# A hybrid encoder layer: one fixed instruction order for the second sweep, its GLA product in three passes, and two-operand work moved from VectorE to GpSimd

## The chip, the cores and the metric

The kernel runs on one core of a Trainium2 chip. A core has a matrix engine (PE, TensorE), a vector engine (DVE, VectorE), an activation engine (ACT, ScalarE), a general engine (POOL, GpSimd), and a queue that issues most DMAs (SP, SyncE). Each works through its own instruction queue in order; semaphores tie them together. The metric is the device time of one execution in microseconds (us).

## The reference, cut to what matters

The layer projects x (2048 x 1024) once and feeds two token mixers: four heads of bidirectional gated linear attention (GLA, decayed scans forward and backward), and four heads of softmax attention with compressed q and kv (MLA). Their gated outputs are joined, projected and normalised.

```python
h = x @ w_in                      # q,k,v,gate,lr_f,lr_b | cq, ckv, kr, gate
# GLA, per chunk and head; b = cumsum(log decay)
o_inter = (q * exp(b)) @ state    # state: decayed sum of k^T v of the chunks before
o = rms_norm(o_fwd + o_bwd, norm_g) * silu(gate)
# MLA
q  = rms_norm(cq) @ w_uq ;  kv = rms_norm(ckv) @ w_ukv   # rope on part of q and on kr
p  = softmax(q_nope k_nope^T + q_rope k_r^T) ;  o = (p @ v) * silu(gate)
x  = layer_norm(alpha * x + concat(o_a, o_b) @ w_out)
```

All is float32. Every large product is computed from splits: a = ah + al, where ah is a rounded copy (`hi`, on ACT) and al the remainder (`lo`, a subtraction of two operands, on DVE or POOL). `mm3` sums ah bh + ah bl + al bh.

## The kernel before, in words

Four stages. **Sweep A** goes over the 16 chunks of 128 tokens from last to first: GLA projections, the part of GLA inside a chunk and the backward state, all stored to HBM (`qd_s`, `oi_s`, `su_s`, and `u_s` for silu of the gate). **Late gates** computes the gates of chunks 15 and 14 and loads the second sweep's weights. **Sweep C**, the second sweep, goes forward, in 8 steps of two chunks; here the change lies. **Attention** then runs 16 blocks of scores, softmax and product, in an order written out by hand (`PLACE`), and ends with the output projection.

In sweep C each chunk c has two halves of work. MLA (`ml_*`, L890 to L950): `ipm` = x times the latent weights (24 matmuls, 448 wide); squares and `rsqrt` (the root comes from Ln and Exp on ACT, then four tiny DVE operations, L160 to L165); normalised `cq`, `ckv`; rope on `kr`; four transposes `tm`, copied to high and low parts; `pqr` and its rope; transposes `tq`. GLA (`gb_*`, L825 to L889): loads `SU`, `qdb`, `oib`, `ub`; the forward state `Sf` times a decay into `Mb` (L846, DVE), `Sf` advanced on POOL (L848, L849); highs and lows of q (`qhb`, `qlb`) and of the joined states (`MMb`, two 64-partition pieces each); the product `Ob` (L865, L866); its norm, the gate (`og`), four transposes `ot` and the store. Per step there are also `pz` (the MLA gate, 96 matmuls, 256 wide) with its silu `gm`, and `pq` (q absorbed into the compressed space, 24 matmuls).

The product reads

```python
mm(Op[:, h], qh[:, h], MM[:, h], start=True, stop=False)        # 256 wide: high and low of MM
mm(Op[:, h, 0], ql[:, h], MM[:, h, 0], start=False, stop=True)  # 128 wide
V.tensor_tensor(oi, Op[:, :, 0], oi, ALU.add)                   # then the second half too
```

so its sum is moved to SBUF (`oib`) by two DVE additions, and the PSUM buffer is free after the second.

Program order is given by hooks between the matmuls (`lat`, `zhooks`); the framework's scheduler then arranges the instructions of each engine by priority and readiness, with a few `after` and `high_priority` hints. PSUM in sweep C is three pools of two buffers: `ip` (ipm), `tr` (transposes, pqr), `gp` (Ob, pz, pq). x of both chunks of a step is held in one pair of tiles (`xch`, `xcl`), so x of the next step can be split only when ipm and pz of this one have read it.

Of the kernel before, what the change touches and what calls it, by code (L numbers as in the profile page):

```python
# [9 lines left out]
F32 = mybir.dt.float32  # L10
# [8 lines left out]
P = 128  # L19
# [81 lines left out]

def _trunc(v, bits):

    m, e = math.frexp(v)
    h = math.ldexp(math.floor(m * 2 ** bits), e - bits)
    return h, v - h


class K:
# [43 lines left out]
    def rsqrt(self, pool, u, n, name):  # L153

        nc = self.nc
        l = pool.tile([P, n], F32, tag=f"rs_l{n}", name=f"{name}_l")
        y = pool.tile([P, n], F32, tag=f"rs_y{n}", name=f"{name}_y")
        t = pool.tile([P, n], F32, tag=f"rs_t{n}", name=f"{name}_t")
        r = pool.tile([P, n], F32, tag=f"rs_r{n}", name=f"{name}_r")
        nc.scalar.activation(l, u, AF.Ln)  # L160
        nc.scalar.activation(y, l, AF.Exp, scale=-0.5)
        nc.vector.tensor_tensor(t, y, y, ALU.mult)
        nc.vector.tensor_tensor(t, t, u, ALU.mult)
        nc.vector.tensor_scalar(t, t, -0.5, 1.5, ALU.mult, ALU.add)
        nc.vector.tensor_tensor(r, y, t, ALU.mult)  # L165
        return r

# [105 lines left out]

    def setup_q(self, w1, ps):

        nc, ins, bc = self.nc, self.ins, self.bc
        for t, n in ((self.gkv_c, "gkv_col"), (self.gn_c, "gn_col")):
            nc.sync.dma_start(t, ins[n])
        gq = bc.tile([P, 2], F32, name="gq")
        nc.sync.dma_start(gq, ins["gq_col"])  # L280
        gkv_b = w1.tile([P, P], F32, tag="ckv", name="gkv_b")
        nc.sync.dma_start(gkv_b, ins["gkv_bc"])
        t1 = w1.tile([P, 2, 512], F32, tag="qa", name="wkr")
        wkT = t1[:, 0].rearrange("p (h l) -> p h l", h=H)
        wqr = t1[:, 1].rearrange("p (c d) -> p c d", c=2)
        nc.sync.dma_start(wqr, ins["wqr"])
        nc.sync.dma_start(wkT, ins["wkT"])
        wqT = w1.tile([P, H, 256], F32, tag="gm", name="wqT")
        nc.sync.dma_start(wqT, ins["wqT"])
        nc.vector.tensor_scalar(gq, gq, QK_SCALE, None, ALU.mult)  # L290
        yield
        for ct in range(2):
            nc.scalar.activation(wqr[:, ct], wqr[:, ct], AF.Copy, scale=gq[:, ct:ct + 1])
        self.hi(self.wqr_h, wqr)
        self.lo(self.wqr_l, wqr, self.wqr_h, "pool")
        for ct in range(2):
            yield
            pa = ps.tile([P, 512], F32, tag="tr", name=f"pabs{ct}")
            for h in range(H):
                nc.tensor.matmul(pa[:, h * P:(h + 1) * P], wqT[:, h, ct * P:(ct + 1) * P], wkT[:, h], start=True,  # L300
                                 stop=True)
            wa = w1.tile([P, H, P], F32, tag="og", name=f"wabs{ct}", bufs=2)
            nc.vector.scalar_tensor_tensor(
                wa, pa.rearrange("p (h l) -> p h l", h=H), gq[:, ct:ct + 1],
                gkv_b[:, None, :].to_broadcast([P, H, P]), ALU.mult, ALU.mult)
            self.hi(self.wabs_h[:, ct], wa)
            self.lo(self.wabs_l[:, ct], wa, self.wabs_h[:, ct], "pool")
        yield
# [195 lines left out]
    def gate(self, c, xh, xl, pool, wide=False):  # L504

        if wide:
            pg = self.gp.tile([P, 2, 512], F32, tag="gp", name=f"ipg{c}")[:, 0]
        else:
            pg = self.ip.tile([P, 512], F32, tag="ip", name=f"ipg{c}")
        for k in range(NK):  # L510
            self.mm3(pg, xh[:, k, 0], xl[:, k, 0], self.wgate[k][0], self.wgate[k][1],
                     start=(k == 0), stop=(k == NK - 1))
        u = self.silu(pool, pg, [P, 512], "gs" if pool is not self.wl else "ub", f"{c}")
        self.store(c).dma_start(self.u_s[c], u)
# [169 lines left out]
    def sweep_c(self):  # L684

        tc, nc, ins = self.tc, self.nc, self.ins
        with ExitStack() as ctx:
            w1 = ctx.enter_context(tc.tile_pool(name="wk2", bufs=1, reuse_waits="tile"))
            sm = ctx.enter_context(tc.tile_pool(name="smc", bufs=2, reuse_waits="tile"))
            ip, tr, gp = self.ip, self.tr, self.gp  # L690
            Wm, Wz = self.Wm, self.Wz
            NST = NCH // 2
            Sf = w1.tile([64, H, P], F32, name="Sf")
            nc.vector.memset(Sf, 0.0)
            xh, xl, split = self.xch, self.xcl, self.split_c
            x2 = lambda t, k: t[:, k].rearrange("p a t -> p (a t)")
            G = [dict(c=c, Sf=Sf, w1=w1, sm=sm, tr=tr, gp=gp) for c in range(NCH)]
            self.gb_load(G[0])
            with tc.high_priority(300):
                self.gb_prep(G[0])  # L700
            setup = self.setup_q(w1, tr)
            next(setup)
            L = None
            for st in range(NST):
                qb, qo = st // 2, (st % 2) * 256
                c0, c1 = 2 * st, 2 * st + 1
                cqT_h = w1.tile([P, 2, 2, P], F32R, tag="cqT_h", name=f"cqT_h{st}")
                cqT_l = w1.tile([P, 2, 2, P], F32R, tag="cqT_l", name=f"cqT_l{st}")
                qrT = []
                cur = [dict(c=c, j=j, st=st, cqT_h=cqT_h, cqT_l=cqT_l, qrT=qrT, w1=w1, sm=sm, tr=tr)  # L710
                       for j, c in enumerate((c0, c1))]
                if st < NST - 1:
                    xs = self.load_x(st + 1, "xc", 2)

                def lat(j, hooks):
                    c = cur[j]["c"]
                    pm = ip.tile([P, 512], F32, tag="ip", name=f"ipm{c}")
                    for k in range(NK):
                        self.mm3(pm[:, :448], xh[:, k, j], xl[:, k, j], Wm[k][0], Wm[k][1],
                                 start=(k == 0), stop=(k == NK - 1))  # L720
# [12 lines left out]
                hooks = {3: [lambda: self.gb_inter(G[c0])]}
                zhooks = {k: [] for k in range(8)}
                if L is not None:
                    P1 = L
                    zhooks[0] += [lambda: self.ml_T(P1)]
                    zhooks[1] += [lambda: self.ml_q(P1)]
                    zhooks[2 if last else 3] += [lambda: self.ml_qT(P1)]
                    zhooks[2 if last else 3] += [lambda: self.absorb(P1), lambda: self.store_qr(P1), lambda: self.gb_out(G[c0 - 1])]  # L740
                else:
                    for k in (1, 3, 5):
                        zhooks[k] += [lambda: next(setup)]
                self.gb_load(G[c1])
                lat(0, hooks)
                self.gb_norm(G[c0])
                if last:
                    self.gb_prep(G[c1])
                    lat(1, {3: [lambda: self.gb_inter(G[c1])]})
                    self.gb_norm(G[c1])  # L750
                    zhooks[2] += [T0]
                    zhooks[3] += [lambda: self.gb_out(G[c0])]
                    zhooks[4] += [q0, T1]
                    zhooks[5] += [qT0, lambda: self.gb_out(G[c1])]
                    zhooks[6] += [q1]
                else:
# [692 lines left out]
```

## Time and profile before

| | |
|---|---|
| median of 3 runs | 1382.49 us (1380.39 to 1384.55) |
| the profiled execution, and its span | 1379.36 us, 1377.5 us |
| mean granted TensorE clock | 0.989 |
| sweep C, first ipm to the first scores | 395.24 to 671.70 us |

The page gives busy time by engine, 40 equal slices of the span, DMA queues, the chain of work that ended last, and the costliest groups of instructions: line, engine, operation, output<-inputs with shapes and count, then busy time and the mean of one in ns, then the idle time of the engine before them with what ended it. A timeline row is start, length, engine, line, operation. Line L123 is the helper `lo`, L117 the helper `hi`, L149 to L151 are `mm3`.

### The profile page before, as it was taken

What the parts mean: (1) busy time and instruction counts of PE and PEld (TensorE: products, weight loads), DVE (VectorE), ACT (ScalarE), POOL (GpSimd) and SP (SyncE); (2) the same over time, 40 slices, a digit from 0 to 9 for tenths busy, and PEclk for the clock granted to TensorE, in tenths of its full rate; (3) what the DMA queues carried; (4) which work ended last, traced back from release to release, by engine and by line L of the source; (5) the groups of instructions that cost most, each with busy time, mean ns of one, the idle gap of its engine ahead of it and who ended that gap; (6) DMA issues with size and microseconds to landing.
All of it is one profiled execution on the core that took longest, in us unless ns stands there. A gap on an engine that the chain in (4) does not pass through costs nothing.

```text
span 1377.5 us, 19847 instructions
## 1 busy us (share of the span) xinstructions
PE 1312.2 (95%) x7056; PEld 1137.9 (83%) x7056; DVE 1013.1 (74%) x1829; ACT 826.2 (60%) x1353; POOL 727.1 (53%) x394
## 2 busy tenths in 40 slices
PE   6899999999998999899999999999999999999997
PEld 6889898989887888888878888888888887787875
DVE  7747755555688777777588888888888888578676
ACT  6555556546575555555577878788888888511110
POOL 3442423232432332232058878889999999745442
PEclk9899999999999999999999999999999999999999
DMA  7222222222384555553711211111112210366973
GB/s 251 81 62 78 62 77 81 81 62 77 107 288 125 183 176 171 165 169 101 238 45 22 57 39 39 39 54 55 54 54 85 65 52 9 87 212 198 182 180 121
DMA packets 108963, 147.38 MB, mean 107 GB/s; under 512 B 17886, under 2 KB 63326, under 8 KB 108864
## 3 DMA queue, kind: packets, MB, share of 16 engines
q1 hardware_dynamic: 99696, 143.98, 35.5%
q0 software_dynamic: 672, 2.10, 0.4%
q10 hardware_dynamic: 8496, 0.03, 0.3%
q8 instruction: 56, 0.92, 0.3%
q14 instruction: 43, 0.35, 0.1%
HBM read 94.93 MB, written 51.15 MB: 106 GB/s over the span
## 4 chain that ended last, share of the span: by engine, by line
PE 50%; DVE 8%; issue 4%; ACT 3%; POOL 2%; DMA 2%; SPq 1%; DVEq 0%; POOLq 0%; ACTq 0%
PE o L149 4%; PE o L151 4%; PE o L150 4%; PE pS L1000 4%; PE pS L1003 4%; PE pS L1002 4%; PE pS L1004 4%; PE pS L1001 4%; PE po L151 1%; PE po L150 1%; PE po L149 1%; DVE MMb L123 1%; PE ipm L149 1%; PE ipm L150 1%; PE ipm L151 1%
## 5 line engine op out<-in xcount | busy, mean ns | idle before, releaser
L123 POOL TENSOR_TENSOR pl<-s,ph 128x1024 fp32r<-128x1024 f32 x128 | 307.1, 2416 | 66.8 <-ACT ph L117 60.4
L1022 DVE TENSOR_TENSOR rm<-pS,rm 128x512 f32<-128x512 f32 x210 | 144.8, 690 | 44.6 <-ACT s L1009 39.5
L1009 ACT ACTIVATE s<-pS 128x1024 f32<-128x1024 f32 x128 | 131.3, 1027 | 67.4 <-PE pS L1004 64.9
L1046 DVE TENSOR_TENSOR s<-s,mb 128x1024 f32<-128x1024 f32 x128 | 151.1, 1212 | 9.2 <-PE mb L1040 9.2
L117 ACT ACTIVATE ph<-s 128x1024 fp32r<-128x1024 f32 x128 | 135.0, 1057 | 16.7 <-PE o L151 16.1
L1050 ACT ACTIVATE s<-s 128x1024 f32<-128x1024 f32 x128 | 131.4, 1050 | 13.5 <-DVE s L1046 13.4
L149 PE MATMUL ipa<-wah,xah 128*128 128x384 f32 (+1 forms) x384 | 131.5, 342 | 6.3 <-ACT wah L117 6.3
L151 PE MATMUL ipa<-wah,xal 128*128 128x384 f32 (+1 forms) x384 | 126.6, 330 | 0.0
L150 PE MATMUL ipa<-wal,xah 128*128 128x384 f32 (+1 forms) x384 | 125.6, 327 | 0.0
L645 POOL TENSOR_TENSOR Us<-Us,cw 128x512 f32<-128x512 f32 x16 | 18.2, 1137 | 202.0 <-DVE Us L642 172.6
L1000 PE MATMUL pS<-qh,ckvT_h 128*128 128x512 f32 x256 | 103.9, 406 | 2.4 <-ACT s L1009 1.7
L149 PE MATMUL o<-ph,vh 128*128 128x512 f32 x256 | 102.6, 401 | 0.0
L151 PE MATMUL o<-ph,vl 128*128 128x512 f32 x256 | 101.3, 396 | 0.0
L1003 PE MATMUL pS<-rh,krs 128*128 128x512 f32 x256 | 101.2, 395 | 0.0
L150 PE MATMUL o<-pl,vh 128*128 128x512 f32 x256 | 101.1, 395 | 0.0
L1002 PE MATMUL pS<-qh,ckvT_l 128*128 128x512 f32 x256 | 100.8, 394 | 0.0
L1004 PE MATMUL pS<-rl,krs 128*128 128x512 f32 x256 | 100.7, 393 | 0.0
L1001 PE MATMUL pS<-ql,ckvT_h 128*128 128x512 f32 x256 | 100.6, 393 | 0.0
L1073 DVE TENSOR_TENSOR ap<-ap,s 128x512 f32<-128x512 f32 x120 | 83.1, 692 | 6.3 <-ACT s L1050 4.4
L149 PEld LDWEIGHTS ipa<-wah,xah 128*128 128x128 f32 x384 | 74.2, 193 | 7.0 <-ACT wah L117 6.3
L123 POOL TENSOR_TENSOR ol<-of,oh 128x512 fp32r<-128x512 f32 x32 | 43.6, 1361 | 68.8 <-ACT oh L117 58.8
L150 PEld LDWEIGHTS ipa<-wal,xah 128*128 128x128 f32 x384 | 74.2, 193 | 1.0 <-DVE wal L123 0.4
(319 smaller groups left out, 3899.1 us busy)
## 6 DMA issues: line engine op xcount, KB each, us to landing
xcf<-xT_dram SPq DMA_DIRECT2D x16, 512.0 KB, 4.1
xr<-x_dram SPq DMA_DIRECT2D x16, 512.0 KB, 6.1
out_dram<-rr SPq DMA_DIRECT2D x32, 256.0 KB, 2.9
xaf<-xT_dram SPq DMA_DIRECT2D x14, 512.0 KB, 4.3
SU<-su_s SPq DMA_DIRECT2D x16, 256.0 KB, 3.5
qdb<-qd_s SPq DMA_DIRECT2D x16, 256.0 KB, 4.1
oib<-oi_s SPq DMA_DIRECT2D x16, 256.0 KB, 2.8
ub<-u_s SPq DMA_DIRECT2D x16, 256.0 KB, 3.0
```

Of the source, the lines that this page charges most:

```text
L117: return nc.scalar.activation(dst, src, AF.Copy).ins
L123: return e.tensor_tensor(dst, src, hi.bitcast(F32), ALU.subtract).ins
L149: mm(out, ah, bh, start=start, stop=False)
L150: mm(out, ah, bl, start=False, stop=False)
L151: mm(out, al, bh, start=False, stop=stop)
L1000: mm(ps[:, e], kh, qh, start=True, stop=False)
L1001: mm(ps[:, e], kh, ql, start=False, stop=False)
L1002: mm(ps[:, e], kl, qh, start=False, stop=False)
L1003: mm(ps[:, e], kr, rh, start=False, stop=False)
L1004: mm(ps[:, e], kr, rl, start=False, stop=True)
L1022: V.tensor_tensor(d["rm"], src[:, e], d["rm"], ALU.max)
L1046: V.tensor_tensor(s, s, d["mb"][:, None, :].to_broadcast([P, 2, QB]), ALU.subtract)
```

## The change

The hooks of sweep C are replaced by a table of places. Each operation of a chunk or step is a small method `c_*`; a place is a number in steps, with one table for the inner steps, one for the first, one for the last. All operations are sorted by step number + place and emitted under `in_order`, which chains the instructions of each of the five engines, SP and POOL included, in exactly that order:

```diff
+            def put(n, st, fn, *a, j=None):
+                last = st == len(steps) - 1
+                p = PLACE_C[n]
+                p = (last and PLACE_C_LAST.get(n)) or (not st and PLACE_C_FIRST.get(n)) or p
+                todo.append((st + (p if j is None else p[j]), len(todo), fn, a))
...
+            last = {}
+            for _, _, fn, a in sorted(todo, key=lambda e: e[:2]):
+                with self.in_order(last):
+                    fn(*a)
```

Sorted, an inner step reads as follows on each engine, from the end of one step's pz to the end of the next (chunk numbers: 9 and 11 odd, 10 even and 12 next):

| engine | order |
|---|---|
| PE | ip 11, pqr 10, Ob 11, ip 12 (three quarters), ot 10, Ob 12, ip 12 (rest), tm 11, pz, tq 10, pz pz, ot 11, pz, pqr 11, pq, pz, tq 11, pz pz, tm 12, pz |
| ACT | xh 12, gm1 gm2 gm3, sqm 11, krT 10, MMh 12, qhb 12, rml 11, sqO 11, krsh 11, xh 13, rgl 11, ckv 11, cq 11, oT 10, sqm 12, ckvTh 11, sqO 12, cqTh 11, qrTh 10, krT 11, vh 11, rgl 12, krsh 12, oT 11, qhb 13, rml 12, MMh 13, qah, cq 12, qrTh 11, ckv 12, cqTh 12, ckvTh 12, vh 12 |
| DVE | gm4, krf 11, ssm 11, oib 11, rmd 11, ss 11, qrf 10, rgd 11, og 11, oib 12, ckvTl 11, krf 12, ss 12, cqTl 11, rgd 12, qrTl 10, og 12, qrf 11, ssm 12, rmd 12, qal, ckvTl 12, cqTl 12, qrTl 11 |
| POOL | xl 12, vl 10, krfa 11, MMl 12, qlb 12, krsl 11, xl 13, qrfa 10, Sf2 13, M 13, Sf1 14, krfa 12, Sf2 14, krsl 12, vl 11, M 14, qrfa 11, MMl 13, Sf1 15, qlb 13 |

`rml`, `rgl` are the ACT parts of rsqrt (of the latents, of GLA), `rmd`, `rgd` the four DVE operations of each; the second letter of a name's end, h or l, is high or low.

The GLA product becomes three accumulating 128-wide passes, the sum is added in PSUM, and `og` reads it there:

```diff
-        mm(Op[:, h], qh[:, h], MM[:, h], start=True, stop=False)
-        mm(Op[:, h, 0], ql[:, h], MM[:, h, 0], start=False, stop=True)
-    V.tensor_tensor(oi, Op[:, :, 0], oi, ALU.add)
-    V.tensor_tensor(oi, Op[:, :, 1], oi, ALU.add)
+        d["Ob"] = self.gp.tile([P, 2, H, P], F32, tag="gp", name=f"Ob{d['c']}")[:, 0]
+            self.mm3(d["Ob"][:, h], d["qh"][:, h], d["ql"][:, h], d["MM"][:, 0, h], d["MM"][:, 1, h])
+        self.nc.vector.tensor_tensor(d["Ob"], d["Ob"], d["oib"], ALU.add)
+            self.nc.vector.scalar_tensor_tensor(d["og"][:, h], d["Ob"][:, h], d["rg"][:, h:h + 1], d["ub"][:, h],
+                                                ALU.mult, ALU.mult)
```

DVE work with two SBUF operands goes to POOL: the decayed state (now written into the lower half of `SU`, so that high and low of the joined state are one operation of 128 partitions each), the lows of q, of the state, of `kr` and of v, and the last addition of both ropes. `Sf` gets two buffers:

```diff
-        V.tensor_tensor(M, Sf, cw[:, 0, :, None].to_broadcast([64, H, P]), ALU.mult)
-        self.lo(ql, qd, qh)
-            self.lo(MM[r, :, 1], m, MM[r, :, 0])
+        self.nc.gpsimd.tensor_tensor(d["SU"][0:64], d.get("Sf", self.Sf), cw[:, 0, :, None].to_broadcast([64, H, P]),
+                                     ALU.mult)
+        self.lo(d["ql"], d["qdb"], d["qh"], "pool")
+        self.lo(d["MM"][:, 1], d["SU"], d["MM"][:, 0], "pool")
+        self.nc.gpsimd.tensor_tensor(d["kr"], d["kr"], d["krt"], ALU.add)
+        self.lo(d["krs"][:, 1], d["kr"][:, 0], d["krs"][:, 0], "pool")
+        self.lo(self.vl[:, d["c"]], d["ckv"], self.vh[:, d["c"]], "pool")
+        self.nc.gpsimd.tensor_tensor(d["qr"], d["qr"], d["qrt"], ALU.add)
```

rsqrt is split in two methods, its four DVE operations unchanged, and the two late gates are stored through POOL's queue:

```diff
+    def rsqrt_b(self, u, y, t, r):
+        nc = self.nc
         nc.vector.tensor_tensor(t, y, y, ALU.mult)
         nc.vector.tensor_tensor(t, t, u, ALU.mult)
         nc.vector.tensor_scalar(t, t, -0.5, 1.5, ALU.mult, ALU.add)
         nc.vector.tensor_tensor(r, y, t, ALU.mult)
...
-        self.store(c).dma_start(self.u_s[c], u)
+        (self.nc.gpsimd if late else self.store(c)).dma_start(self.u_s[c], u)
```

The absorbed weights of the first step (`su_*`: pb, wa, wh, wl) get places too, among them two lows `wl` on POOL.

More of the change, by code (lines that the diff above doesn't have):

```diff
@@ L99 @@
 )
+SETUP_C = ("lset", "wS", "wH", "wL", "pb0", "wa0", "wh0", "wl0", "pb1", "wa1", "wh1", "wl1")
+STEP_C = ("gm1", "gm2", "gm3", "gm4", "sgm", "pq", "qah", "qal", "sqa", "sqr")
+CHUNK_C = ("lx", "xh", "xl", "lS", "lq", "lo", "lu", "sqm", "ssm", "rml", "rmd", "cq", "ckv", "krf", "krfa",
+    "krsh", "krsl", "vh", "vl", "tm", "cqTh", "cqTl", "ckvTh", "ckvTl", "krT", "pqr", "qrf", "qrfa",
+    "tq", "qrTh", "qrTl", "Sf1", "Sf2", "M", "qhb", "qlb", "MMh", "MMl", "Ob", "oib", "sqO", "ss",
+    "rgl", "rgd", "og", "ot", "oT", "soT")
@@ new lines @@
+PLACE_C_LAST = dict(
+    ipa=(-0.122, 0.173),
+    ipb=(0.005, 0.222),
+    ipc=(0.048, 0.346),
+    ipd=(0.136, 0.359),
+    Ob=(0.052, 0.335),
+    tm=(0.517, 1.085),
+    pqr=(0.79, 1.216),
+    tq=(0.922, 1.591),
+    ot=(0.781, 0.958),
+    xh=(-0.308, 0.01),
+    qhb=(-0.012, 0.11),
+    MMh=(-0.115, 0.189),
+    sqO=(0.149, 0.369),
+    rgl=(0.313, 0.409),
+    sqm=(0.191, 0.45),
+    rml=(0.323, 0.696),
+    cq=(0.4, 0.932),
+    ckv=(0.411, 0.982),
+    vh=(0.43, 1.348),
+    krsh=(0.406, 0.617),
+    cqTh=(0.651, 1.091),
+    ckvTh=(0.582, 1.166),
+    krT=(0.666, 1.188),
+    qrTh=(1.07, 1.646),
+    oT=(0.826, 1.152),
+    oib=(0.116, 0.359),
+    ss=(0.185, 0.397),
+    rgd=(0.379, 0.504),
+    og=(0.382, 0.532),
+    ssm=(0.261, 0.685),
+    rmd=(0.39, 0.918),
+    krf=(0.221, 0.603),
+    cqTl=(0.668, 1.147),
+    ckvTl=(0.604, 1.395),
+    qrf=(0.82, 1.25),
+    qrTl=(1.083, 1.646),
+    xl=(-0.246, 0.163),
+    M=(-0.221, -0.033),
+    Sf1=(-0.739, -0.705),
+    Sf2=(-0.66, 0.215),
+    qlb=(0.047, 0.252),
+    MMl=(-0.019, 0.273),
+    krfa=(0.337, 0.612),
+    krsl=(0.426, 0.995),
+    vl=(0.529, 2.449),
+    qrfa=(0.903, 1.578),
+    lS=(-0.691, -0.22),
+    lq=(-0.57, -0.29),
+    lo=(0.076, 0.069),
+    lu=(-0.018, 0.233),
+    lx=(-1.163, -0.556),
+    soT=(0.846, 1.94),
+    pz=(0.556, 0.573, 0.625, 0.692, 0.811, 0.827, 1.023, 1.199),
+    gm1=1.25,
+    gm2=1.283,
+    gm3=1.31,
+    gm4=1.419,
+    sgm=1.49,
+    pq=1.577,
+    qah=1.777,
+    qal=2.479,
+    sqa=3.483,
+    sqr=1.75,
+)
@@ L271, in run @@
             self.attention()
[L274 to L308, printed above, removed]
     def rope_angles(self, pos_i, pos_f, invf, hpi):
@@ new lines, in c_krT, with c_pqr, c_qrf @@
+    def c_krT(self, d):
+        self.hi(self.kr[:, d["c"], :P], d["tm"][:, 3])
+    def c_pqr(self, d):
+        pq = d["pqr"] = self.tr.tile([P, 512], F32, tag="tr", name=f"pqr{d['c']}")
+        s, j = d["step"], d["j"]
+        for ct in range(2):
+            self.mm3(pq[:, :256], s["cqT_h"][:, ct, j], s["cqT_l"][:, ct, j], self.wqr_h[:, ct], self.wqr_l[:, ct],
+                     start=(ct == 0), stop=(ct == 1))
+    def c_qrf(self, d):
+        d["qr"] = self.w1.tile([P, H, 64], F32, tag="qrf", name=f"qrf{d['c']}")
+        d["qrt"] = self.rope(d["qr"], d["pqr"][:, :256].rearrange("p (h d) -> p h d", h=H), d["c"], H)
```

633 lines of the change are left out of this document (395 added, 238 removed).

## The prediction

> **What bounds the kernel now.** I read the page first, then busy time by stretches, the waits of the sweep, and its timeline. The page:
>
> ```profile
> span 1377.5 us, 19847 instructions
> PE 1312.2 (95%) x7056; PEld 1137.9 (83%) x7056; DVE 1013.1 (74%) x1829; ACT 826.2 (60%) x1353; POOL 727.1 (53%) x394
> ```
>
> TensorE (PE) is the bound over the whole span. The change touches the second sweep alone, so what it can give is PE time lost there. Busy time in three stretches of the sweep (first step, the steady steps, the last two):
>
> ```profile
> 395.00:437.00 42.00, 36.32 (x230) 33.35 (x229) 36.25 (x73) 25.92 (x58) 16.52 (x11) 0.96 0.61 200
> 437.00:607.00 170.00, 155.14 (x1076) 145.91 (x1075) 125.58 (x364) 95.48 (x242) 51.94 (x30) 0.98 0.54 174
> 607.00:672.00 65.00, 61.94 (x444) 58.75 (x444) 45.04 (x153) 36.03 (x97) 11.12 (x6) 0.97 0.43 137
> ```
>
> The columns after the length are PE, weight load, DVE, ACT, POOL, then the granted clock. PE is idle 14.9 of 170 us in the steady steps, and the clock is below 1. DVE has the most work beside PE, POOL is nearly empty. The waits of the steady stretch say why PE idles:
>
> ```profile
> POOL Sf L848 <- DVE Mb L846: 66.2, 7, 13.8
> PE Ob L865 <- DVE MMb L123: 9.7, 5, 2.1
> ```
>
> The GLA product waits for the lows of its operands, late on DVE. Now the PE rows that give the lengths:
>
> ```profile
> 395.24 0.36 PE L149 MATMUL ipm<-wmh,xch 128*128 128x448 f32 x1
> ...
> 400.10 0.36 PE L149 MATMUL ipm<-wmh,xch 128*128 128x448 f32 x1
> ...
> 436.54 0.28 PE L149 MATMUL pz<-xch,wzh 128*128 128x256 f32 x1
> ...
> 471.44 0.28 PE L149 MATMUL pz<-xch,wzh 128*128 128x256 f32 x1
> 471.56 0.28 PE L150 MATMUL pz<-xcl,wzh 128*128 128x256 f32 x1
> ...
> 492.37 0.22 PE L866 MATMUL Ob<-MMb,qlb 128*128 128x128 f32 x1
> 492.43 0.34 PE L865 MATMUL Ob<-MMb,qhb 128*128 128x256 f32 x1
> 492.60 0.23 PE L866 MATMUL Ob<-MMb,qlb 128*128 128x128 f32 x1
> ...
> 607.46 0.28 PE L149 MATMUL pz<-xch,wzh 128*128 128x256 f32 x1
> ...
> 671.70 0.48 PE L1000 MATMUL pS<-qh,ckvT_h 128*128 128x512 f32 x1
> ```
>
> 436.54 and 607.46 are the first pz products of steps 1 and 6: five steps in 170.9 us, 34.2 us each. The first step and lead-in take 436.54 - 395.24 = 41.3, the end 671.70 - 607.46 = 64.2; 276.5 in all. Start to start, a 448-wide product takes 0.2025 us (24 of them from 395.24 to 400.10), a 256-wide one 0.12, and a wide-narrow GLA pair 0.23, 0.115 a matmul.
>
> **What PE needs after the change.** A step is 48 x 0.2025 = 9.7 (ip), 96 x 0.12 = 11.5 (pz), 36 x 0.12 = 4.3 (pq and pqr), 20 transposes x 0.115 (taken as the GLA matmuls, as wide) = 2.3, and the GLA products. These go from 8 to 12 matmuls a chunk. A 128-wide matmul in this stream is not shown: 0.06 and 0.17 (the starts at 492.37, 492.43, 492.60) bound it; I take 0.115, the pair's mean, since each loads its own weights. 24 x 0.115 = 2.8, **0.9 us more a step than before** (bounds: 0.4 less, and 2.2 more). Sum 30.5 us: against 34.2, 3.7 are there to win in a steady step. The whole sweep is 8 x 30.5 plus some 2 for the sixteen absorb matmuls (at 0.115 and a little to start), 246 against 276.5: **at most 30 us to win**, if no engine is late.
>
> **What leaves DVE.** The rows of its low halves and others over the sweep:
>
> ```profile
> L123 POOL TENSOR_TENSOR xcl<-xcf,xch 128x1024 fp32r<-128x1024 f32 x13 | 31.4, 2418 | 64.1 <-ACT xch L117 42.8 <-PE Ob L866 14.2 <-PE Ob L865 7.0
> L123 DVE TENSOR_TENSOR MMb<-SU,MMb 64x512 fp32r<-64x512 f32 x16 | 27.5, 1722 | 0.5
> L880 DVE SCALAR_TENSOR_TENSOR og<-oib,rg_r,ub 128x128 f32<-128x128 f32 x64 | 20.1, 345 | 0.2
> L123 DVE TENSOR_TENSOR MMb<-Mb,MMb 64x512 fp32r<-64x512 f32 x16 | 13.6, 848 | 0.0
> L867 DVE TENSOR_TENSOR oib<-Ob,oib 128x512 f32<-128x512 f32 x16 | 11.0, 687 | 7.5 <-PE Ob L866 7.5
> L872 DVE TENSOR_REDUCE ss<-og 128x4 f32<-128x512 f32 x16 | 10.9, 683 | 3.1 <-ACT og L870 2.9
> L117 ACT ACTIVATE qhb<-qdb 128x512 fp32r<-128x512 f32 x16 | 10.1, 633 | 1.2 <-PE Ob L865 1.2
> L822 ACT ACTIVATE gm<-gm 128x1024 f32<-128x1024 f32 x8 | 8.5, 1063 | 0.0
> L897 ACT ACTIVATE sqm<-ipm 128x256 f32<-128x256 f32 x16 | 6.0, 373 | 3.6 <-PE ipm L151 3.5
> L160 ACT ACTIVATE rm_l<-ssm 128x2 f32<-128x2 f32 x16 | 3.2, 199 | 17.8 <-DVE ssm L900 17.8
> ```
>
> The two MMb lows alone are 41 us of DVE; the second oib add (as the first, 11 us) goes with the second half of PSUM. ACT saves one 0.63 us copy a chunk. That work is hidden today except where Ob waits, so I count it only through those waits, in the 3.7 above. POOL takes, per chunk, xl 2.42, then qlb, MMl, Sf1, Sf2 and M at 1.0 to 1.3 (rows below), and four small ones that no row shows on POOL (bounds: in proportion to their size, 0.15 to 0.65, and 1.29, a full 128x512; I take 0.3 to 0.7): 10, or 20 a step. That is below 30.5, so POOL is no bound by its load. The two late gate stores go from SP's queue to POOL's, two issues ahead of the first step: nothing; if POOL were late by then, 1 us once. SP carries the same loads and stores in a new order:
>
> ```profile
> qdb<-qd_s SPq DMA_DIRECT2D x16, 256.0 KB, 4.1
> ```
>
> It lands in 4.1 us, and by the walk below it is issued 7 us ahead of its use: nothing. With that cover gone a late load would cost up to 4.1 us, once a step; the range holds that.
>
> **What becomes late.** Rows of DVE and POOL where they meet:
>
> ```profile
> 407.56 1.03 POOL L848 TENSOR_TENSOR Sf<-Sf,cw 64x512 f32<-64x512 f32 x1 [5.28 <-DVE Mb L846]
> 408.55 1.29 POOL L123 TENSOR_TENSOR wqr_l<-wkr,wqr_h 128x512 fp32r<-128x512 f32 x1
> 410.79 1.27 POOL L849 TENSOR_TENSOR Sf<-Sf,SU 64x512 f32<-64x512 f32 x1 [0.95 <-DMA SU<-su_s]
> ...
> 493.32 2.41 POOL L123 TENSOR_TENSOR xcl<-xcf,xch 128x1024 fp32r<-128x1024 f32 x1 [7.13 <-PE Ob L866]
> ...
> 513.24 1.03 POOL L848 TENSOR_TENSOR Sf<-Sf,cw 64x512 f32<-64x512 f32 x1 [13.76 <-DVE Mb L846]
> 514.35 1.61 POOL L849 TENSOR_TENSOR Sf<-Sf,SU 64x512 f32<-64x512 f32 x1
> ```
>
> ```profile
> 408.00 1.85 DVE L163 TENSOR_TENSOR rm_t<-rm_t,ssm 128x2 f32<-128x2 f32 x1
> 410.09 0.16 DVE L165 TENSOR_TENSOR rm_r<-rm_y,rm_t 128x2 f32<-128x2 f32 x1
> 411.48 0.62 DVE L873 TENSOR_SCALAR ss<-ss 128x4 f32<-128x4 f32 x1
> ...
> 494.23 1.22 DVE L823 TENSOR_TENSOR gm<-pz,gm 128x1024 f32<-128x1024 f32 x1 [0.20 <-ACT gm L822]
> ...
> 513.42 1.40 DVE L123 TENSOR_TENSOR qlb<-qdb,qhb 128x512 fp32r<-128x512 f32 x1
> ```
>
> A two-element product on DVE, 0.16 us otherwise, began at 408.00 inside a POOL operation and ended at 409.85, when the next POOL operation too had ended. Those two POOL operations had no gap between them. At 513.42 the POOL pair had one (514.27 to 514.35, the second needs the first) and DVE got in between, holding the second back (1.61 for 1.28). The scalar operation at 411.48 waited as well. The one at 494.23, with one operand in PSUM, did not. So DVE and POOL exclude each other when DVE reads two operands from SBUF, and who runs without a gap keeps the other out. The change takes the large such operations off DVE, but **leaves the four tiny ones of each rsqrt (rmd, rgd) and ss's scalar step**, four rsqrts a step, beside a POOL that is then busy 20 us of a step and not 10.
>
> The second thing is a hold: Ob's sum now stays in PSUM until og has read it. pool gp has two buffers, and pz of a step takes the one that Ob of the odd chunk before leaves. So pz waits for the whole norm of that chunk.
>
> Walk a steady step from 0, the end of pz. PE does ip of the odd chunk (4.9) and pqr (0.7). ACT does xh and three gm passes, DVE gm4: xh 1.1 (as wide as gm), 3 x 1.06 and 1.2, 5.6 with the handovers, so Ob runs from 5.6 to 7.0 and oib ends at 7.9. PE goes on with ip of the next chunk, ot, Ob, tm, and wants pz at 14.1. Free of POOL, DVE and ACT have square 0.63, ss 0.68 and 0.16, rgl 2 x 0.2, rgd 4 x 0.16, og 4 x 0.345 = 1.4, with rmd, qrf and xh between: og ends near 12.8, inside 14.1. Now with POOL: sqm (two squares, the wide one 0.37, with a read of the sum behind each, some 1.0) waits for ip and ends at 6.1, krT and MMh follow to 7.0, and POOL starts MMl, qlb, krsl, xl: 1.3 + 1.3 + 0.3 + 2.4, to 12.4, each ready before the last one ends. rmd is ready at 7.9, inside MMl. At best half of it slips in ahead of xl (xh ends at 9.9, krsl too); the rest comes after 12.4. Behind it in DVE's queue stand ss and qrf, to 14.7. There POOL gets qrfa and Sf2, which need not wait for each other, to 16.8. rgd gets two of its four operations in before qrfa and two after Sf2, where M needs Sf2 and leaves a gap: 17.2. og ends at 18.6. **pz starts at 18.7, not 14.1: 4.6 us of PE a step** (bounds: 0, if rsqrt finds gaps; 6.9, if the last three operations each wait for another of POOL's, to 21.0). Behind pz on PE stand tq, ot, pqr and pq, and for these wait qrTh, oT and qah on ACT; all of it moves back with pz. What a pause of PE does to its clock, a stretch just behind one of the waits for MMb shows:
>
> ```profile
> 501.00:506.00 5.00, 5.00 (x22) 4.61 (x22) 4.02 (x21) 2.32 (x11) 0.00 (x0) 0.67 0.55 181
> ```
>
> A clock of 0.67 for 5 us costs 1.65; I take 1.5 once a step (bounds 0 and 3). In the second half PE has 16.4 us of its own work, which covers the same waits of the even chunk.
>
> Whether the scalar step inside rmd (128x2) waits is shown for 128x4 only, at 411.48. The Trainium skill's GPSIMD Engine Reference, in its section Specifications, puts contention on VectorE instructions in a two-port mode or with two SBUF inputs; by it that step waits too, and an rgd that must wait once more would end some 1 us later, near 1405 for the kernel, against the 1398 below. No row here shows that shape beside POOL.
>
> **The sum.** Steady: 30.5 + 4.6 + 1.5 = 36.6 against 34.2, 2.4 x 5 = +12. First: 34.6 of PE work (246 less five steps and the 59 of the end, which holds two pz, three pq, ip and Ob, five pqr and the transposes) + 6.1 + 2.5 for the two wl operations that POOL has ahead of step 1 = 43.2 against 41.3, +2. End: 59 + 6.1 = 65.1 against 64.2, +1. In all +15. The profiled execution took 1379.36, giving 1394; the median shown is 1382.49, 3.1 higher, giving **1398**.
>
> **Rivals.** *The norm chain is in time* (other side): the tiny operations fall into POOL's gaps, and og ends by 14.1. For it: without POOL there are 1.3 us in hand, and POOL itself waits for DVE's krf and qrf, which opens gaps. Against it: MMh stands ahead of rml on ACT, so rmd always meets POOL's run. Then 246 plus some 9 for first and last steps and small waits is 255, 21 less: 1361; it decides when rmd and rgd together lose under about 4 us a step. *POOL starves DVE further*: pz at 21.0 (+2.3 a step) and rgd, rmd of the even chunk late for pq and tm by a little over 1: +27 over eight steps, 1425. For it: 408.00 lost two whole operations. Against: the second half has slack. *No difference*: losses happen to equal today's 34.2 a step, 1382.
>
> **How the numbers follow.** Forecast 0.36 (1389 to 1411), further starved 0.23, in time 0.35, no difference 0.06. The range reaches from a little under the in-time case, 1356, to 1425. A measurement of this kernel tells some 0.3% (4 us); the first two cases are slower, 0.59, in time is faster, 0.35, same 0.06.
>
> **What would show it.** Right: pz's first matmul idle 4 to 5 us a step, ended by DVE og; DVE rm_t, rg_t far above 0.16 us on average; PE idle on tiles MMb gone; POOL near 20 us a step; a step, from pz to pz, some 36.6 us. Wrong: pz waits for nothing, steps near 31 us, clock at 1.00 through the sweep; or another wait, such as pz for xcl, is the long one.

## The result and the profile after

The changed kernel took 1405.99 us (median; 1403.38 to 1409.09) against 1383.52 us for the kernel before on the same chip: a ratio of 1.0167, 95% interval 1.0138 to 1.0196. It is slower. The profiled execution took 1404.66 us. From its page, the span and busy time by engine:

```profile
span 1402.9 us, 19978 instructions
PE 1326.3 (95%) x7120; PEld 1155.5 (82%) x7120; DVE 989.3 (71%) x1683; ACT 814.6 (58%) x1338; POOL 809.1 (58%) x509
```

DVE is busy 24 us less and POOL 82 us more (the waits shown below count as DVE's busy time); PE has 64 matmuls more (the third pass). Busy time in the first step and in the steady steps of the second sweep (columns as before; the granted clock is the third from the end):

```profile
395.00:447.00 52.00, 41.29 (x255) 38.47 (x254) 35.00 (x61) 27.53 (x67) 35.47 (x33) 0.89 0.47 154
447.00:630.00 183.00, 163.42 (x1118) 156.35 (x1118) 112.71 (x270) 87.74 (x228) 98.84 (x100) 0.94 0.47 152
```

In the steady steps PE idles 19.6 of 183 us (14.9 of 170 before), and the clock is 0.94 (0.98 before). POOL's 98.84 us are 19 a step. What PE waited for in the sweep (engine, line, releaser: us in total, times, longest):

```profile
PE pz L368 <- DVE og L1214: 15.9, 6, 4.1
PE tm L1089 <- ACT cq L1059: 11.0, 8, 2.0
PE pabs L940 <- DMA wqT<-wqT_dram: 5.5, 1, 5.5
```

No wait for the GLA product's lows (`MMb`) is left. In its place stand pz, held by og of the GLA norm, and tm, held by the normalised cq. The PE rows that give the lengths:

```profile
397.81 0.36 PE L368 MATMUL ipm<-wmh,xch 128*128 128x448 f32 x1
...
446.77 0.58 PE L368 MATMUL pz<-xch,wzh 128*128 128x256 f32 x1 [4.08 <-DVE og L1214]
...
487.30 0.58 PE L368 MATMUL pz<-xch,wzh 128*128 128x256 f32 x1 [2.37 <-DVE og L1214]
...
504.96 0.37 PE L368 MATMUL ipm<-wmh,xch 128*128 128x448 f32 x1
...
519.90 0.44 PE L1089 MATMUL tm<-ident,cq 128*128 128x128 f32 x2 [1.23 <-ACT cq L1059]
...
522.93 0.39 PE L368 MATMUL pz<-xch,wzh 128*128 128x256 f32 x1 [2.37 <-DVE og L1214]
...
630.39 0.58 PE L368 MATMUL pz<-xch,wzh 128*128 128x256 f32 x1 [2.37 <-DVE og L1214]
...
694.67 0.48 PE L1287 MATMUL pS<-qh,ckvT_h 128*128 128x512 f32 x1
```

First step 446.77 - 397.81 = 49.0 us (41.3 before), five steps 183.6 (170.9), end 64.3 (64.2): 296.9 against 276.5. The first of the five steps took 40.5 us, the other four 35.8 each. The profiled execution is 25.3 us longer than that of the kernel before; the sweep accounts for 20.4. The rest lies outside it, where the code is the same, and is of the size by which runs differ there (among the kernels below the sweep begins anywhere from 393.4 to 397.2 us).

Why og is late is written in one step's DVE rows:

```profile
513.59 0.50 DVE L382 TENSOR_TENSOR rm_t<-rm_y 128x2 f32<-128x2 f32 x1 [0.86 <-ACT rm_y L377]
514.12 1.22 DVE L383 TENSOR_TENSOR rm_t<-rm_t,ssm 128x2 f32<-128x2 f32 x1
515.38 0.25 DVE L384 TENSOR_SCALAR rm_t<-rm_t 128x2 f32<-128x2 f32 x1
515.66 2.29 DVE L385 TENSOR_TENSOR rm_r<-rm_y,rm_t 128x2 f32<-128x2 f32 x1
...
519.39 0.15 DVE L382 TENSOR_TENSOR rg_t<-rg_y 128x4 f32<-128x4 f32 x1
519.58 0.72 DVE L383 TENSOR_TENSOR rg_t<-rg_t,ss 128x4 f32<-128x4 f32 x1
520.33 1.19 DVE L384 TENSOR_SCALAR rg_t<-rg_t 128x4 f32<-128x4 f32 x1
521.55 0.16 DVE L385 TENSOR_TENSOR rg_r<-rg_y,rg_t 128x4 f32<-128x4 f32 x1
521.75 1.13 DVE L1214 SCALAR_TENSOR_TENSOR og<-Ob,rg_r,ub 128x128 f32<-128x128 f32 x4
```

and POOL's in the same stretch:

```profile
514.03 1.29 POOL L342 TENSOR_TENSOR qlb<-qdb,qhb 128x512 fp32r<-128x512 f32 x1
515.28 0.32 POOL L342 TENSOR_TENSOR krs<-krf,krs 128x64 fp32r<-128x64 f32 x1
515.56 2.38 POOL L342 TENSOR_TENSOR xcl<-xcf,xch 128x1024 fp32r<-128x1024 f32 x1
519.55 0.72 POOL L1124 TENSOR_TENSOR qrf<-qrf,rope 128x256 f32<-128x256 f32 x1 [1.62 <-DVE rg_t L382]
520.24 1.25 POOL L1165 TENSOR_TENSOR Sf<-Sf,SU 64x512 f32<-64x512 f32 x1
```

The product at 514.12, two numbers a partition, ends at 515.34, when qlb is over (515.32); rm_r, begun at 515.66 beside xl, ends at 517.95, when xl is over (517.94). From the first start to the last end the four operations of rmd took 4.36 us; in e1 below, where nothing keeps them out, they take 0.77.

### The profile page after: what moved, and what is told of

Read it like the earlier page. It is cut to its first block, busy times and chain, and to the rows that moved or that the text cites. A ratio compares the mean times of both kernels' runs of the same rounds, so it can differ in the third digit from the quotient of the medians.

```text
span 1402.9 us, 19978 instructions
## 1 busy us (share of the span) xinstructions
PE 1326.3 (95%) x7120; PEld 1155.5 (82%) x7120; DVE 989.3 (71%) x1683; ACT 814.6 (58%) x1338; POOL 809.1 (58%) x509
## 3 DMA queue, kind: packets, MB, share of 16 engines
q1 hardware_dynamic: 99408, 143.46, 34.6%
## 4 chain that ended last, share of the span: by engine, by line
PE 51%; DVE 10%; DMA 5%; ACT 2%; POOL 2%; issue 2%; SPq 0%; DVEq 0%; POOLq 0%; ACTq 0%
PE pS L1287 4%; PE pS L1290 4%; PE pS L1289 4%; PE pS L1291 4%; PE pS L1288 4%; PE o L368 4%; PE o L369 4%; PE o L370 4%; PE pz L368 2%; PE pz L370 2%; PE pz L369 2%; DMA xr<-x_dram 2%; DMA of<-ob_s 1%; DVE rm_r L385 1%; DVE rr L1666 1%
## 5 line engine op out<-in xcount | busy, mean ns | idle before, releaser
L368 PE MATMUL pz<-xch,wzh 128*128 128x256 f32 x256 | 80.4, 314 | 16.1 <-DVE og L1214 15.9
```

The lines of the kernel that those rows point to most:

```text
L368: mm(out, ah, bh, start=start, stop=False)
```

## The experiments

All ratios are to runs of the kernel before on the same chip. "Step" is the mean of the four steps from the third pz to the seventh. "Waits" are the main waits of PE in a typical one of them. Nothing of the computation is left out in any of them.

| kernel | median, us | ratio (95%) | step | waits of PE in a step |
|---|---|---|---|---|
| before | 1383.52 | 1 | 34.3 | Ob for MMb 2.0 |
| changed | 1405.99 | 1.0167 (1.0138 to 1.0196) | 35.8 | pz for og 2.4, tm for cq 1.2 |
| e1, scratch in PSUM | 1354.67 | 0.9835 (0.9807 to 0.9863) | 30.3 | none |
| e7, rm only | 1388.14 | 1.0072 (1.0050 to 1.0095) | 34.2 | pz for og 2.2 |
| e8, rg only | 1386.76 | 1.0049 (1.0025 to 1.0072) | 34.3 | tm 1.3, pz 0.7 |
| e4, lows on DVE | 1391.48 | 1.0098 (1.0071 to 1.0126) | 34.1 | Ob for qlb 2.0 |
| e6, e1 and e4 | 1387.85 | 1.0021 (0.9998 to 1.0043) | 33.9 | Ob for qlb 2.0 |
| e5, before, lows on POOL | 1391.07 | 1.0092 (1.0061 to 1.0122) | 34.7 | Ob for MMb, pqr, tm, ot 3.0 in all |
| e10, before, scratch in PSUM | 1378.43 | 0.9991 (0.9966 to 1.0016) | 34.2 | Ob for MMb 1.8 |
| e11, no hold | 1403.39 | 1.0126 (1.0092 to 1.0161) | 35.7 | ot for cqTl 2.9, tm 1.2 |
| e12, e1 and SBUF dose | 1379.81 | 0.9966 (0.9949 to 0.9983) | 32.0 | pz for og 1.4 |
| e13, e1 and PSUM dose | 1364.56 | 0.9853 (0.9824 to 0.9883) | 30.5 | 1.0 in all of them together |
| e2, early weights | 1400.81 | 1.0166 (1.0138 to 1.0195) | 35.8 | as changed |
| e3, e1 and e2 | 1355.83 | 0.9837 (0.9814 to 0.9860) | 30.3 | none |

The theory was that of the prediction: DVE operations with two SBUF operands wait out POOL's operations, the tiny ones of rsqrt above all. The rivals were that the fixed order or the hold of Ob in PSUM costs the time by itself, or that one of the moves does.

**The tiny operations' operands (e1).** ScalarE writes its first estimate y once more, into PSUM, and the product t lives there too; rm uses the unused end of ip's bank, rg and the sum of ss the unused half of Ob's buffer:

```diff
+        y2 = y
+        if ps is not None:
+            y2, t = ps[:, 0:n], ps[:, 4:4 + n]
+            nc.scalar.activation(y2, l, AF.Exp, scale=-0.5)
...
-        nc.vector.tensor_tensor(t, y, y, ALU.mult)
+        nc.vector.tensor_tensor(t, y2, y, ALU.mult)
...
-        d["rm"] = self.rsqrt_a(self.sm, d["ssm"], 2, f"rm{d['c']}")
+        d["rm"] = self.rsqrt_a(self.sm, d["ssm"], 2, f"rm{d['c']}", d["pm"][:, 448:512])
...
-        V.tensor_reduce(ss, d["og"], AX.X, ALU.add)
-        V.tensor_scalar(ss, ss, 1.0 / P, RMS_EPS, ALU.mult, ALU.add)
+        s8 = d["Ob2"][:, 8:8 + H]
+        V.tensor_reduce(s8, d["og"], AX.X, ALU.add)
+        V.tensor_scalar(ss, s8, 1.0 / P, RMS_EPS, ALU.mult, ALU.add)
```

> The changed kernel with the scratch of both rsqrt chains in PSUM: ScalarE writes its first estimate y a second time into PSUM (one more activation of about 0.2 us for each rsqrt), and the DVE ops of the two chains and the scalar step of ss each get one operand in PSUM. The order of the work, the hold of Ob in PSUM until og and the place of every other op stay. Theory (DVE ops with two SBUF operands wait out the POOL op that runs): the ops of rmd and rgd fall from 0.7-1.3 us to about 0.2 us each, pz no longer waits for og (2.37 us a step) nor tm for cq (1.23 us a step), the steady step falls from 36.7 us to 31-33 us, and the whole to 1365-1380 us. Rival (the fixed order and the PSUM hold cost the time, whatever these small ops take): the step stays at 36 us or more and the time within 5 us of the changed kernel's 1406 us.

Measured: 1354.67 us, better than the theory's own range. Busy time of this kernel over 194 us of steady steps, and one rm of it:

```profile
446.00:640.00 194.00, 194.00 (x1433) 188.73 (x1432) 95.20 (x355) 115.85 (x327) 118.87 (x124) 1.00 0.58 189
```

```profile
523.72 0.17 DVE L386 TENSOR_TENSOR ipm<-ipm,rm_y 128x2 f32<-128x2 f32 x1 [0.93 <-ACT ipm L381]
...
524.33 0.16 DVE L389 TENSOR_TENSOR rm_r<-rm_y,ipm 128x2 f32<-128x2 f32 x1
```

PE is busy all 194 us at clock 1.00, in the same fixed order, with the same hold and the same work on POOL. A step is 30.3 us, PE's own need. So with these operations out of the way neither order nor hold nor place costs anything in a steady step; the whole loss there came through them. This version beats both kernels.

**One chain at a time (e7, e8).** The same edit for one rsqrt alone.

> The changed kernel with PSUM scratch for the rsqrt of ip (rm) alone; the rsqrt of the GLA output (rg) and the scalar step of ss stay in SBUF. Theory (rmd stands ahead of ss and rgd in DVE's queue and is the longest of the two, 4.4 us for four operations; rgd then adds 2 to 3 us): pz's wait for og falls from 2.4 us a step to 0-1 us, tm's wait for cq goes, the step is 31-33 us, the time 1358-1375 us. Rival (the wait of og is set by rg's own operations): pz still waits 1.5 us or more a step, the step is 33.5-35 us, the time 1375-1395 us.

> The changed kernel with PSUM scratch for the rsqrt of the GLA output (rg, with the scalar step of ss) alone; rm stays in SBUF. Theory: rmd still ends at about 12.4 us of the step, since ss, rgd and og stand behind it in DVE's queue; rgd takes 0.7 us in place of 2.3; pz's wait falls from 2.4 to about 1 us a step and tm's wait of 1.2 us for cq stays; the step is 33-35 us, the time 1375-1392 us. Rival (rg alone sets the wait): pz waits for nothing, step 31-32 us, time under 1368 us.

Measured: e8 as its theory had it (34.3 us a step, 1386.76). For e7 the theory fell and the rival holds: pz still waits 2.2 us. Alone the edits gain 13 and 16 us of the changed kernel's loss (the differences of the ratios times 1383), together 46. With rm quick, rg in e7 comes some 3 us earlier in the step and meets a POOL operation it had missed:

```profile
508.56 1.96 DVE L386 TENSOR_TENSOR rg_t<-rg_y 128x4 f32<-128x4 f32 x1
```

```profile
508.14 2.37 POOL L342 TENSOR_TENSOR xcl<-xcf,xch 128x1024 fp32r<-128x1024 f32 x1
```

The first of rg's products, 0.15 us in the changed kernel, takes 1.96 here, until xl is over. A wait taken from one operation was handed to the next one in DVE's queue.

**Dose and control (e12, e13).** On e1, two more tiny products ahead of each rsqrt, their result unused; the two kernels differ only in where one operand lies:

```diff
+        if y2 is not y:
+            nc.vector.tensor_tensor(z, y, y, ALU.mult)    # e13: z, y2, y
+            nc.vector.tensor_tensor(z, z, y, ALU.mult)    # e13: z, y2, z
```

> The changed kernel with PSUM scratch for both rsqrt chains (1354.7 us, step 30.3 us), and in front of each rsqrt's DVE operations two more tiny products of which both operands lie in SBUF; nothing uses their result. Theory (such an operation waits out the POOL operations beside it): the added operations take 0.4-1.6 us each on average in place of 0.16, og comes 2-4 us later where it had 1.1 us in hand, pz waits for og again, the step goes to 31.5-35 us and the time to 1362-1392 us. Rival (what counts is only DVE's own time): 0.16-0.2 us each, the step stays at 30.3-30.6 us and the time within 4 us of 1355 us.

> The same two added products per rsqrt, but with one operand of each in PSUM: the control for the kernel beside it. Theory: 0.16-0.2 us each, step 30.3-30.8 us, time 1353-1360 us. Rival (any further operation in DVE's fixed order delays og, wherever its operands lie): step and time as in the kernel with the SBUF operands.

The added products of e12, over 194 us (group rows: count, then busy us and the mean of one in ns):

```profile
L389 DVE TENSOR_TENSOR rm_z<-rm_z,rm_y 128x2 f32<-128x2 f32 x12 | 11.7, 971 | 0.4
L388 DVE TENSOR_TENSOR rm_z<-rm_y 128x2 f32<-128x2 f32 x12 | 7.8, 646 | 7.2 <-ACT rm_y L377 7.2
L389 DVE TENSOR_TENSOR rg_z<-rg_z,rg_y 128x4 f32<-128x4 f32 x11 | 5.8, 528 | 0.4
L388 DVE TENSOR_TENSOR rg_z<-rg_y 128x4 f32<-128x4 f32 x11 | 4.1, 372 | 0.5
```

and two of the four of e13 (the others take 156 and 162 ns):

```profile
L389 DVE TENSOR_TENSOR rm_z<-ipm,rm_z 128x2 f32<-128x2 f32 x13 | 2.1, 159 | 0.5
L388 DVE TENSOR_TENSOR rm_z<-ipm,rm_y 128x2 f32<-128x2 f32 x13 | 2.1, 158 | 7.9 <-ACT ipm L381 7.9
```

0.37 to 0.97 us against 0.16, and a ratio of 0.9966 against 0.9853; e13's interval overlaps e1's. The same number of operations in the same order costs nothing that these runs resolve, or 1.1%, by the place of an operand. The theory holds: e12 lies in its ranges, save the one product at 0.37 us. e13 has the step (30.5) and the lengths expected, but its 1364.56 us lies above the 1353 to 1360. Its sweep takes 255.8 us against e1's 253.7; the rest lies outside the sweep, on a chip where the kernel before took 1383.81 us and not 1378.38 as beside e1.

**Order and place (e4, e6, e5, e10).** The four lows that the change put on POOL go back to DVE, in the changed kernel (e4) and in e1 (e6); or to POOL in the kernel before (e5); and e1's edit of rsqrt alone goes into the kernel before (e10):

```diff
-        self.lo(d["MM"][:, 1], d["SU"], d["MM"][:, 0], "pool")
+        self.lo(d["MM"][:, 1], d["SU"], d["MM"][:, 0])          # e4, e6; likewise qlb, krs, vl
```

> The changed kernel with its fixed order, but with the four ops that the change moved to POOL in the second sweep (krs low, vl, qlb, MMl) back on DVE; POOL keeps the rest. Theory (the loss comes from the long POOL ops that stand beside the tiny DVE ops): rmd meets no MMl and no qlb on POOL, only xcl, rgd still meets Sf and SU; the stall of pz for og falls from 2.4 us to under 1.5 us a step, the step from 36.7 us to 32-35 us, and the time to 1378-1398 us. Rival (the order and the hold of Ob until og set the step, place does not matter): DVE takes 2-3 us more in each step, og comes later, the step is 37-39 us and the time 1406-1420 us.

> The changed kernel with PSUM scratch for both rsqrt chains and with the four lows (krs, vl, qlb, MMl) back on DVE: the fixed order with neither the move to POOL nor the waits of the tiny operations. Theory (once the tiny operations no longer wait, the move to POOL is worth what it was meant for): Ob waits for qlb on DVE as in the kernel with the lows on DVE, the step is 32-34 us, the time 1365-1385 us. Rival (the fixed order alone does it, the place does not matter): step 30.3-31 us, time within 5 us of 1355 us.

> The kernel before, with the scheduler's own order, and only the place changed: the lows qlb, MMb (both halves), krs and vl of the second sweep go from DVE to POOL. Theory (work on POOL keeps DVE's small operations of two SBUF operands out, so the place by itself gives little or a loss): the rsqrt operations of DVE take 0.5 us or more each in place of 0.2, the waits of the GLA product for its lows do not fall by more than half, and the time is 1375-1400 us beside 1380. Rival (place alone is the gain and the fixed order spoils it): the step falls from 34.2 us to 31-32 us and the time to 1355-1365 us.

> The kernel before, with only the scratch of both rsqrt chains in PSUM (the same edit as in the changed kernel with PSUM scratch; the second half of Ob's own PSUM tile and the free end of ip's tile are used). Theory (before the change POOL has 10 us a step and the GLA product waits for lows that are late on DVE, not for the tiny operations): the step stays between 33 and 34.5 us and the time within 6 us of the kernel before. Rival (the tiny operations' waits cost the kernel before as much, and the gain of 50 us in the changed kernel has nothing to do with the change): the step falls to 31-32 us, the time by 15 us or more.

The wait of PE over 194 us of e6, and what the place alone does to one of rsqrt's operations in e5:

```profile
PE Ob L370 <- DVE qlb L342: 9.8, 5, 2.0
```

```profile
L163 DVE TENSOR_TENSOR rm_t<-rm_t,ssm 128x2 f32<-128x2 f32 x11 | 12.7, 1158 | 0.2
```

Measured: e4 in the theory's ranges, and pz no longer waits for og in its inner steps; but Ob waits 2.0 us for qlb in its place, which the theory had not named. e6 by its step (33.9) as the theory had it, its 1387.85 us just above the range. e5 inside its range, though only one of rsqrt's operations went above 0.5 us (the one shown; it is 0.16 in those steps of the kernel before), and PE's waits for MMb went to POOL's MMb instead, at 1.0 us a step where it was 2.0. e10 is no different from the kernel before, where these operations take 0.16 us in the steady steps anyway. So the place of the four lows alone loses 0.9%, and the PSUM scratch alone gives nothing. The change without that place (its order, the third pass and the other work moved to POOL) loses 1% (e4) or, with the scratch, gains nothing (e6): there the scratch is worth 0.8%. The place is worth 1.9% beside the scratch (e6 to e1) and costs 0.7% without it (e4 to the changed kernel). All together give 1.65%. Whether the fixed order is needed for that is not shown: the scheduler's order with both scratch and place was not tried, nor the order by itself.

**The hold (e11).** The sum goes to SBUF, so pz need not wait for og:

```diff
-        self.nc.vector.tensor_tensor(d["Ob"], d["Ob"], d["oib"], ALU.add)
+        d["os"] = d["Ob"]
+        if d["c"] < NCH - 2:
+            d["os"] = self.w1.tile([P, H, P], F32, tag="os", name=f"os{d['c']}")
+        self.nc.vector.tensor_tensor(d["os"], d["Ob"], d["oib"], ALU.add)
```

> The changed kernel, but in all chunks save the last two the sum of Ob and oib is written to SBUF, so that Ob's PSUM buffer is free for pz when that one sum is done, long before og. The square and og then read SBUF, and og has two SBUF operands and waits for POOL too. Theory (the late norm costs where something waits for it; the hold only makes pz the one that waits): pz's 2.4 us for og go, ot waits for og in its place or not at all, tm's wait of 1.2 us for cq stays or grows to 2 us as og's four operations take 0.45 us or more each ahead of it; the step falls from 35.8 us to 33-35 us, the time to 1380-1400 us. Rival (the hold is the whole loss): no wait of PE over 0.3 us a step, step 30.3-31.5 us, time 1355-1365 us.

```profile
PE ot L1223 <- DVE cqT_l L342: 14.3, 5, 3.1
PE tm L1089 <- ACT cq L1059: 8.1, 6, 2.0
```

Pz's wait goes, and its 2.4 us come back as ot's 2.9 for cqTl, which stands behind og in DVE's queue. The rival (the hold is the loss) falls; but the step (35.7) did not fall to 33 to 35 us as the theory had it either, and 1403.39 us lies above the theory's 1380 to 1400. The hold chose who waits, not how long.

**The first step (e2, e3).** One number, the place of the weight loads on SP:

```diff
-    lset=-0.576,
+    lset=-1.2,
```

> The changed kernel with one number changed: the loads of the second sweep's weights are put ahead of the loads of the first step's u on SP. Theory (the first stretch is 8 us longer than before because the load of wqT queues behind the load of ub, which waits for a late store): the wait of 5.5 us of pabs for the load of wqT goes, and the half clock after it; the first stretch falls from 49.0 us to 40-44 us, the steady step stays at 36.7 us, and the time falls by 5-10 us to 1396-1401 us. Rival (the load is only one of several late things there, such as xch or the ramp of the clock): the wait of pabs turns into another of the same length and the time stays within 2 us of the changed kernel.

> Both edits at once: the rsqrt chains' scratch in PSUM and the weights of the second sweep loaded ahead of its first u. Theory (two separate causes, one in the steady step, one in the first stretch): the gains add, the time is 1356-1375 us and so below the 1383 us of the kernel before. Rival (one late chain behind both): no better than the better of the two by more than 2 us.

Measured in e2: 1400.81 us, inside the theory's range, but on a chip where the kernel before takes 1378.38: the ratio is that of the changed kernel (1.0166), and the first stretch takes 49.4 us, not 40 to 44. From PE's waits in e2's first step:

```profile
PE Ob L368 <- ACT MMb L336: 3.8, 1, 3.8
...
PE pabs L940 <- DMA wqT<-wqT_dram: 1.3, 1, 1.3
```

The wait for wqT falls from 5.5 to 1.3 us, and Ob now waits 3.8 us for MMb: the rival's case. e3 is no different from e1 (0.9837 beside 0.9835), again as its rival had it; the wait for MMb is 4.6 us there. Behind it stands, in e3's DVE and ACT rows:

```profile
400.27 4.13 DVE L342 TENSOR_TENSOR wzl<-wzr,wzh 128x512 fp32r<-128x512 f32 x3
```

```profile
403.05 0.63 ACT L336 ACTIVATE wzh<-wzr 128x512 fp32r<-128x512 f32 x1 [3.59 <-DVE wzl L342]
404.38 0.61 ACT L336 ACTIVATE MMb<-SU 128x512 fp32r<-128x512 f32 x1
```

Three splits of weights, of which one took 0.62 us at 394.51, took 4.13: they began beside POOL's M, which qlb followed without a gap, and qlb was over at 402.46, 1.9 us before they ended. ACT waited for them, and MMb's high stood behind in ACT's queue. That reads as the same exclusion, but no run here took it away.

## Why the prediction was right

Time and sign: 1398 forecast, 1405.99 measured, slower as forecast, by the mechanism forecast. Step by step:

- *PE needs 30.5 us a step* (its terms add to 30.6). e1: 30.3, with PE never idle. In e1 the twelve GLA matmuls of a chunk take 1.29 us from first start to the next product, 0.11 each against the 0.115 taken.
- *What leaves DVE counts only through PE's waits; POOL 20 us a step is no bound.* The waits for MMb are gone and POOL has 19 us a step, its small operations at 0.32 to 0.73 us. In e1 it has as much, and PE does not wait.
- *DVE and POOL exclude each other when DVE reads two SBUF operands.* e12 against e13. The step that rested on one row (an operand in PSUM escapes) is now shown by every operation of e1.
- *The walk.* From the end of pz (504.96): rmd ready at 8.6 (forecast 7.9), done at 13.0 (after 12.4), rgd done at 16.7 (17.2), og at 17.9 (18.6), pz at 18.0 (18.7). PE's loss is 2.37 + 1.23 = 3.6 us, not 4.6: tm takes a third of it, ahead of pz, which the walk did not name, and pz would have come at 14.4, not 14.1. One premise did not hold in the inner steps: that a run of POOL operations without a gap keeps DVE out. MMl, qlb, krsl and xl follow one another without a gap, and rmd still got one operation in at each seam (514.12, 515.38, 515.66); three of the four, not half, began ahead of xl. As the last one then waited out xl, rmd ended about where the walk had it; that the two ways agree there is luck.
- *The clock, 1.5 us a step.* 35.8 - 30.3 - 3.6 = 1.9. The drop, one stretch behind the wait:

```profile
518.00:523.00 5.00, 1.40 (x9) 0.77 (x7) 4.83 (x14) 2.51 (x10) 3.29 (x4) 1.00 0.33 100
523.00:528.00 5.00, 5.00 (x30) 5.00 (x31) 4.45 (x12) 2.06 (x8) 3.76 (x6) 0.66 0.83 268
```

- *The sum.* End 64.3 (65.1 forecast). Steady 36.7 on the mean of five (36.6), but made of 40.5 and four of 35.8: the first of them stands behind a wait of 4.1 us, not 2.4, and runs with more of the clock gone (0.50 from 447 to 452 us), and tm waits 2.0 us in it. That the mean agrees to 0.1 us is luck.
- *The term that was mis-sized: "First: 34.6 of PE work + 6.1 + 2.5".* It measured 49.0, not 43.2. In e1, where the stall and its clock (the 6.1) are gone, the first step still takes 43.5, so the front of it costs 8.9, not the 2.5 put down for two operations on POOL; the stall, at 49.0 - 43.5 = 5.5, was sized right. The front was priced by POOL's load alone, and SP's new order was put at nothing from the row of qdb. In fact PE waits 5.5 us for the load of wqT there, and from 405 to 415 us the granted clock is 0.50. In e1 the wait is 5.2 us, and the clock of 0.50 and then 0.74 in the two stretches of 5 us behind it is worth another 3.8: 9.0 in all. The load alone is not the cause: with it out of the way (e2) another wait takes its place and the time is the same. The kernel before, too, has 5.6 us of PE's waits in its first step, for which the sum had no term.
- *Scalar operations inside rmd.* The text left open whether a 128x2 one waits. It does, in e8:

```profile
418.60 1.23 DVE L388 TENSOR_SCALAR rm_t<-rm_t 128x2 f32<-128x2 f32 x1
```

```profile
418.51 1.29 POOL L342 TENSOR_TENSOR qlb<-qdb,qhb 128x512 fp32r<-128x512 f32 x1
```

  It ended at 419.83, with qlb (419.80). In the steady steps it met only the short krs (0.25). So the rule cited there from the Trainium skill's GPSIMD Engine Reference, Specifications, was right on this shape, while the later end of rgd priced with it did not come: rgd was done at 16.7. That 1405.99 lies beside the 1405 of that sentence is luck.
- *The rivals.* "The norm chain is in time" was worth 1361 by the text, and e1, which makes it so, took 1354.67 (by its ratio, 0.9835 of 1383.52, some 1361). Its bound of 4 us of loss in rmd and rgd was passed: against e1, rmd loses 3.6 and rgd 1.6.

The Trainium skill's SBUF — State Buffer, in its section Summary: rules for kernel authors, says that a VectorE operation with two SBUF inputs, issued second, blocks until the GpSimd operation that runs, if it reads SBUF, has finished. The trace agrees for most (2.29 us beside xl). In a few places it is more than that. In e8 a product begun at 416.34 beside one POOL operation lasted 2.22 us, to the end of the next, which had followed without a gap.

```profile
416.34 2.22 DVE L387 TENSOR_TENSOR rm_t<-rm_t,ssm 128x2 f32<-128x2 f32 x1
```

```profile
416.25 1.29 POOL L342 TENSOR_TENSOR wqr_l<-wkr,wqr_h 128x512 fp32r<-128x512 f32 x1
417.51 1.03 POOL L1166 TENSOR_TENSOR Sf<-Sf,cw 64x512 f32<-64x512 f32 x1
```

In e8's last step one such product, begun at 638.73, lasted 5.13 us, through the whole run of MMl, qlb, krsl and xl, as the prediction's premise would have it. What decides between one operation and several, no run here shows.

## What to carry to other kernels

Before work is moved from VectorE to GpSimd, look at what stays on VectorE: a two-element operation there can cost as much as the whole GpSimd operation beside it, and what stands behind it in the queue pays. An operand in PSUM takes it out of the conflict (0.16 us against 0.4 to 1.0), for one more operation on ScalarE. Take all such operations out of a chain, or expect a part of the gain (13 and 16 of 46 us here): a wait removed from one can fall to the next.

## What the runs showed that was not expected

Pauses of PE of some 2 us in a step cost nearly twice their length; one of 1.4 us did not. In e8 PE waits 1.33 and 0.72 us within 3 us of each step, and the step loses 4.0 (34.3 - 30.3). The clock in e8 behind these two waits:

```profile
508.00:513.00 5.00, 3.87 (x21) 3.64 (x22) 3.60 (x14) 3.08 (x11) 4.84 (x6) 0.75 0.62 200
513.00:518.00 5.00, 5.00 (x41) 5.00 (x40) 2.60 (x10) 2.12 (x9) 2.39 (x4) 0.91 0.49 170
```

That is 1.7 us on top of 2.05. In e7 one wait of 2.2 us costs 3.9, with a clock of 0.73 from 513 to 518 us behind it. In e12 a single wait of 1.43 us left the clock at 1.00, and the step loses 1.7:

```profile
507.63 0.39 PE L368 MATMUL pz<-xch,wzh 128*128 128x256 f32 x1 [1.43 <-DVE og L1224]
```

```profile
510.00:515.00 5.00, 5.00 (x45) 5.00 (x44) 2.83 (x12) 2.08 (x8) 2.40 (x4) 1.00 0.59 208
```

e5 idles some 3.3 us a step in small pieces with the clock at 1.00. The Trainium skill's TensorE: Matmul & The Clock Gate, in Why this matters for your kernels, warns of idle gaps over some 3 us; here 2.2 us, or two gaps adding to 2.05, were enough, and 1.43 were not.
